# A hybrid decoder layer on one core: stores and side work placed later, groups started one pair of tiles earlier

## The chip, the core and the metric

The kernel runs on one core of a Trainium2 chip. Its engines work at the same time, each through its own instructions in order: TensorE (PE; its weight loads are PEld), VectorE (DVE), ScalarE (ACT), GpSimd (POOL) and SyncE (SP), which here issues the DMA transfers. The metric is device time in microseconds (us); lower is better.

## What is computed

One layer of a decoder over 2048 tokens of width 1024, in float32. After an RMS norm one input projection (1024 to 8320 columns) feeds a recurrent mixer with a matrix state (RWKV-7), a short convolution and a causal pooling over windows of 2, 4, 8 and 16, and three gates for each channel. Each branch is projected, the three are merged by the gates, one output projection follows, then a norm and the residual.

```python
def _rwkv7_step(state, inp):
    r_t, w_t, k_t, v_t, a_t, b_t = inp
    sa = jnp.einsum('bhvk,bhk->bhv', state, a_t)
    state = (state * w_t[:, :, None, :] + sa[..., None] * b_t[:, :, None, :]
             + v_t[..., None] * k_t[:, :, None, :])
    y_t = jnp.einsum('bhvk,bhk->bhv', state, r_t)
    return state, y_t
...
        h = rms_norm(x, pre_norm_w[l])
...
        p = h @ w_cat
        p_rwkv, p_conv, p_pool, p_gate = jnp.split(
            p[..., :N_IN],
            [N_RWKV_IN, N_RWKV_IN + N_CONV_IN, N_RWKV_IN + N_CONV_IN + N_POOL_IN], axis=-1)
        p_rwkv = token_shift(p_rwkv, mu_shift[l])
...
        y_b = short_conv_branch(p_conv, conv_w[l])
        y_c = pool_branch(p_pool, pool_w[l], pool_scale[l])
        ys = jnp.stack([y_a, y_b, y_c], axis=0)
        proj = jnp.einsum('nbsc,ncd->nbsd', ys, w_branch[l])
        gates = jax.nn.sigmoid(p_gate.reshape(bsz, slen, N_BRANCH, D_MODEL))
        merged = jnp.einsum('bsnd,nbsd->bsd', gates, proj)
        out = merged @ w_out[l]
        x = x + rms_norm(out, post_norm_w[l])
```

## The kernel before

Large products are done in float32 accuracy by splitting both operands into a high and a low part, three matmuls for each of four slices, so that one *product* is twelve matmuls of 128x128 by 128x512 (L182 to L184). The weights come as raw pieces by DMA (L149), ScalarE casts the high part (L141), GpSimd subtracts for the low part (L143). The token axis is done in two halves of 1024.

Two tiles of output channels by two blocks of tokens are computed together with seven products in place of eight (the class `Pair`): B11, T1, T2, B21, B22, T3 and T4. T4 is left over to the next pair, where it comes after T1. VectorE evicts with additions at L247 (after B21), L251 (after B22) and L255 (after T3); T4 adds onto the bank that L255 reads, and the next T1 takes the bank that L247 reads. For the sums of weights GpSimd adds (L212).

`execute` runs the program of jobs. A job is a generator that yields after each product; at each yield `supply` prepares coming weights (raw pieces five products ahead, sums three, splits two) and each *side* of the job is advanced by its rate. The jobs: eight pairs and a single tile of projections for the first half (60 products and the low-rank ones, L527 to L529), then for each half eight pairs of the convolution branch (`conv_tile`: a convolution pair, L864 to L869, and a gating pair, L848 and L875), four of pooling (`pool_tile`, additions at L898) and twelve of gates (L950), with the second half's projections after the first half's gates; then eight merge tiles of six products for each half (L981 on VectorE, L985 on GpSimd), and eight pairs of output rows (`out_pair`).

The sides: `rwkv_groups`, eight groups of 128 tokens for each half, each 25 steps long. A group multiplies its chunk matrices (L691, L694, L699), stores a triangle (L704) and loads it by rows (L718), inverts it in 15 pairs of operations (L730, L731) in four batches, one step apart, stores and reloads the result (L738, L740), transposes it (L745, Td), completes the inverse (L753 to L792) and passes the state on (L804 to L833). The following group's head (L561 to L616) and the group before's tail (L624 to L652) run in the same steps. Other sides: `stage_ops` (norm and transposes of the second half's input, L434 to L465), `stage_sums` (L460 to L466), `mix_pooled` (L930 to L943), and the plans that load and split coming operands (L333, L339, L340). `side.finish` runs what is left of a side at once.

PE, DVE, ACT and POOL execute in the order in which the code writes their work; SyncE is not in that list, and its order is the scheduler's:

```python
    with tc.manual_schedule(engines={mybir.EngineType.PE, mybir.EngineType.DVE, mybir.EngineType.Activation,
                                     mybir.EngineType.Pool}):
```

`out_pair` scales a row by its norm and adds the input row (L1023, L1024), for two blocks of 512 columns, once both blocks of the row are there; the norm is three small operations on GpSimd (L470 to L472) after the squares on ScalarE (L1015).

Of the kernel before, what the change touches and what calls it, by code (L numbers as in the profile page):

```python
# [53 lines left out]
def trunk_kernel(ctx, tc, x, pre_norm_w, post_norm_w, w_in, mu_shift, rwkv_w0, rwkv_w_up,  # L54
# [261 lines left out]

    def new_op(o):

        hi = hp_.tile([P, HK, BLK], F32R, tag="hh", name=f"h{o}")
        lo = hp_.tile([P, HK, BLK], F32, tag="hl", name=f"l{o}")  # L320
        return [hi[:, k, :] for k in range(HK)], [lo[:, k, :].bitcast(F32R) for k in range(HK)]
# [104 lines left out]
    def stage_ops(half):  # L426

        for j in range(TH // P):
# [14 lines left out]
            yield  # L443
            for q in range(2):
                t = work("hB")[:, :BLK]
                transposed(xs[q], q, t)
                sp.dma_start(hR[q, b][:, :, c0 * P:(c0 + 1) * P], t.rearrange("p (k t) -> p k t", k=HK))
# [3 lines left out]
    def stage_sums(block, dst):  # L451

        for k in range(2 * HK):
# [7 lines left out]
            yield  # L461
            for o, out_, a, b in (("T1", B[0, 0], B[0, 1], B[0, 0]), ("T3", B[0, 1], B[1, 1], B[0, 1]),
                                  ("T2", B[1, 1], B[1, 1], B[0, 0]), ("T4", B[1, 0], B[1, 0], B[1, 1])):
                dve.tensor_tensor(out_, a, b, ALU.subtract)
                sp.dma_start(dst[o][:, k, cs], out_)  # L465
# [9 lines left out]
    def rwkv_cols(half, c, b, val):  # L475
# [14 lines left out]
        sp.dma_start((rD, kD, vD, zD)[kind][:, i, t0:t0 + BLK], sh)  # L490
# [14 lines left out]
    def rwkv_single(half, h, c):  # L505
# [8 lines left out]
        def sink(b, val):  # L514
# [6 lines left out]
            def products(upw):  # L521
                (uh, ul) = upw
                for n, bias in enumerate((hw0, ha0)):
                    ns = half_of(n)
                    for i in range(NCT):
# [6 lines left out]
                        sp.dma_start(loraD[n][:, i, t0:t0 + BLK], o)  # L532
# [86 lines left out]
    def group_tail(g, by, v):  # L619
# [29 lines left out]
        dve.tensor_tensor(flat(y), flat(y), flat(v), ALU.add)  # L649
        pool.tensor_tensor(flat(y), flat(y), flat(z), ALU.mult)  # L650
        yield
        sp.dma_start(yD[0][:, :, t0:t0 + P], it(y))  # L652
# [10 lines left out]
    def rwkv_group(g, head, before, following):  # L663
# [37 lines left out]

        nd = tc.dram_tile([4, 2 * NCT, 32, 32], F32, name=f"nd{g}")
# [3 lines left out]
        BKs = rp.tile([P, 2, 2 * NCT, 64], F32, tag="BKs", name="BKs")  # L706
        for n in range(2):
            bt = rk_bank()
            quarters(bt, BK[:, n])
            act.copy(BKs[:, n], bt.rearrange("p (a k) -> p a k", k=64))  # L710
            if n:

                ndf = nd.rearrange("q a s t -> (q a) s t")
                NBt = rp.tile([P, 16, 16], F32, tag="BK", name="NB")
                for u in range(2):
                    us = slice(u * 16, u * 16 + 16)
                    for g2 in range(2):
                        sp.dma_start(NBt[(2 * u + g2) * 32:(2 * u + g2) * 32 + 32], ndf[:, us, us])  # L718
                bb = rk_bank()
                for i in range(NCT):  # L720
                    pe.matmul(bb[:, i * P:(i + 1) * P], qones[:, i], it(r)[:, i], start=True, stop=True)
                dve.tensor_tensor(flat(v), bb, flat(v), ALU.mult)
            yield from step()
# [4 lines left out]
        for j in range(15):  # L728
# [122 lines left out]
    def conv_tile(half, h, i):  # L851
# [22 lines left out]
        def gated(e, b, val, _):  # L874
            dve.tensor_tensor(ys[b], ys[b], silu2(val) if e else val, ALU.mult)  # L875
            done.append(b)
            if done.count(b) == 2:
                t0 = half * TH + b * BLK
                sp.dma_start(yD[1][:, i, t0:t0 + BLK], ys[b])
# [3 lines left out]
    def pool_tile(half, h, i):  # L883
        w = WINDOWS[i]

        def sink(e, b, val, u):
            t0 = half * TH + b * BLK
            if e:
                sp.dma_start(yD[2][:, i, t0:t0 + BLK], silu2(val))
# [23 lines left out]
            sp.dma_start(pD[:, i, t0:t0 + BLK], pl[:, :BLK])  # L913
# [3 lines left out]
    def mix_pooled(half):  # L917

        for i in range(NCT):
            pw = work("pw")[:, :P]  # L920
            sp.dma_start(pw, pool_w[i])
            for b in range(NB):
# [20 lines left out]
                sp.dma_start(yD[2][:, i, t0:t0 + BLK], z)  # L943
# [3 lines left out]
    def gate_pair(half, h, n, d):  # L947
        def sink(e, b, val, tile_):
# [3 lines left out]
            sp.dma_start(gD[n][d + e, :, t0:t0 + BLK], t)  # L952
# [10 lines left out]

    def merge_tile(half, ys, d):

        def body():
            acc = [None] * NB
            for n in (1, 2, 0):
                gs = []
                for b in range(NB):  # L970
                    t0 = half * TH + b * BLK
                    gt = work("g")
                    sp.dma_start(gt[:, :BLK], gD[n][d, :, t0:t0 + BLK])
                    gs.append(gt[:, :BLK])
# [11 lines left out]
            for b in range(NB):  # L986
                t0 = half * TH + b * BLK
                sp.dma_start(mD[:, d, t0:t0 + BLK], acc[b])
# [13 lines left out]
    def out_pair(ops, post, j):  # L1002
# [10 lines left out]
        def sink(e, b, val, _):  # L1013
# [5 lines left out]
            for b in range(2):  # L1019
# [216 lines left out]
    def execute(first):  # L1236
        for n, entry in enumerate(program):
# [44 lines left out]
```

## Time and profile before

| | |
|---|---|
| median of three runs | 2371.32 us (2369.45 to 2372.01) |
| the profiled execution | 2369.79 us |
| its span, first to last instruction | 2368.1 us |
| mean granted TensorE clock | 0.952 |
| busy: PE, PEld | 2195.8, 1768.5 us |
| busy: DVE, ACT, POOL | 1403.7, 888.3, 1371.6 us |
| DMA | 313 MB, mean 132 GB/s |

The chip grants TensorE's clock at one of two levels, 2.4 GHz (1.00 in the profile) or 1.2 GHz (0.50); a stretch shows the mean. Busy matmuls are pipelined: at full clock a new one of 512 columns starts every 0.23 us while each is shown with some 0.40 us. A row of a timeline has start, duration, engine, line, operation and tiles; in brackets stands the idle time of that engine before it, and what ended it.

### The profile page before, as it was taken

Reading aid. Unit: us, or ns where it says so; the run is one execution under the profiler, and the core shown is the slowest. Engines: PE = TensorE matmul, PEld = TensorE weight load, DVE = VectorE, ACT = ScalarE, POOL = GpSimd, SP = SyncE. Lnnn points to the kernel's source line nnn. Section 1 sums busy time; section 2 is a strip of 40 time slices with the busy share of each in tenths; the row PEclk is TensorE's granted clock in tenths of the full one; section 3 lists DMA queues with packets and bytes.
Section 4 is the critical chain, followed back from the end, with each engine's and each line's share of the span. In section 5 each row is a group of like instructions: output and inputs, shape, how many; then the busy total and the mean of one; then the engine's idle time right before and its main releaser. Section 6 shows DMA issues by size and latency. Waiting matters only on the chain. (4 is left out here: it accounts for less than half of the span.)

```text
span 2368.1 us, 47007 instructions
## 1 busy us (share of the span) xinstructions
PE 2195.8 (93%) x18514; PEld 1768.5 (75%) x18514; DVE 1403.7 (59%) x2182; ACT 888.3 (38%) x1745; POOL 1371.6 (58%) x1137
## 2 busy tenths in 40 slices
PE   4999989989999998899999998999999898998887
PEld 4788877767787876678877776877777687887775
DVE  7413786777756537554495767766674653527454
ACT  5444432433434345344433333343343311214332
POOL 7567764655646554436775545565574444556774
PEclk7989999999999998889999999999999899999998
DMA  3343322343565336444321323455555746865442
GB/s 101 111 135 119 94 65 74 101 123 101 146 191 158 103 93 203 133 147 140 117 84 54 89 67 99 126 174 148 159 157 177 210 134 176 272 187 183 138 129 71
DMA packets 441207, 313.11 MB, mean 132 GB/s; under 512 B 105557, under 2 KB 362778, under 8 KB 440986
## 3 DMA queue, kind: packets, MB, share of 16 engines
q1 hardware_dynamic: 440986, 310.12, 43.6%
q8 instruction: 145, 2.38, 0.4%
q14 instruction: 76, 0.62, 0.1%
HBM read 206.08 MB, written 103.94 MB: 131 GB/s over the span
## 5 line engine op out<-in xcount | busy, mean ns | idle before, releaser
L143 POOL TENSOR_TENSOR wl<-ws,wh 128x512 fp32r<-128x512 f32 x484 | 680.4, 1409 | 508.5 <-ACT wh L141 489.7
L182 PE MATMUL ch<-hT,wh 128*128 128x512 f32 x864 | 359.3, 416 | 49.9 <-DVE p L255 33.3
L141 ACT CAST wh<-ws 128x512 fp32r<-128x512 f32 x484 | 298.8, 618 | 264.0 <-POOL ws L212 102.8
L183 PE MATMUL ch<-lT,wh 128*128 128x512 f32 x864 | 347.7, 402 | 0.0
L184 PE MATMUL ch<-hT,wl 128*128 128x512 f32 x864 | 347.2, 402 | 0.3 <-POOL wl L143 0.3
L184 PE MATMUL mm<-hB,wl 128*128 128x512 f32 x600 | 238.3, 397 | 8.5 <-POOL wl L143 8.5
L182 PE MATMUL mm<-hB,wh 128*128 128x512 f32 x600 | 244.5, 407 | 1.0 <-ACT p L298 1.0
L182 PEld LDWEIGHTS ch<-hT,wh 128*128 128x128 f32 x864 | 168.8, 195 | 94.6 <-issue 54.6
L183 PE MATMUL mm<-lB,wh 128*128 128x512 f32 x600 | 237.7, 396 | 0.0
L143 POOL TENSOR_TENSOR wl<-s,wh 128x512 fp32r<-128x512 f32 x72 | 97.8, 1358 | 186.5 <-ACT wh L141 175.5
L212 POOL TENSOR_TENSOR ws<-ws,s 128x512 f32<-128x512 f32 x144 | 201.3, 1398 | 0.1
L184 PEld LDWEIGHTS ch<-hT,wl 128*128 128x128 f32 x864 | 168.4, 195 | 38.4 <-POOL wl L143 0.8
L183 PEld LDWEIGHTS ch<-lT,wh 128*128 128x128 f32 x864 | 168.9, 195 | 33.1
L985 POOL TENSOR_TENSOR g<-g 128x512 f32<-128x512 f32 x64 | 87.7, 1374 | 116.0 <-DVE g L981 110.7
L184 PEld LDWEIGHTS mm<-hB,wl 128*128 128x128 f32 x600 | 114.8, 191 | 34.5 <-POOL wl L143 9.4
L182 PEld LDWEIGHTS mm<-hB,wh 128*128 128x128 f32 x600 | 114.8, 191 | 28.1 <-issue 1.5
L182 PE MATMUL mm<-hT,wh 128*128 128x512 f32 x296 | 124.0, 419 | 10.4 <-DVE Ttmp L730 10.4
L183 PEld LDWEIGHTS mm<-lB,wh 128*128 128x128 f32 x600 | 114.8, 191 | 22.6
L184 PE MATMUL ch<-hB,wl 128*128 128x512 f32 x288 | 116.6, 405 | 14.1 <-POOL wl L143 14.1
L182 PE MATMUL ch<-hB,wh 128*128 128x512 f32 x288 | 119.7, 416 | 6.6 <-DVE g L981 4.9
L212 POOL TENSOR_TENSOR ws<-ws 128x512 f32<-128x512 f32 x72 | 104.8, 1456 | 31.3 <-DMA ws<-in_w_in 31.3
L730 DVE TENSOR_TENSOR Ttmp<-NB,Tt 128x120 f32<-128x120 f32 (+14 forms) x240 | 115.4, 481 | 11.0 <-DMA NB<-nd 4.4
(270 smaller groups left out, 4668.1 us busy)
## 6 DMA issues: line engine op xcount, KB each, us to landing
ws<-in_w_in SPq DMA_DIRECT2D x260, 256.0 KB
g<-gD SPq DMA_DIRECT2D x96, 256.0 KB
gD<-p SPq DMA_DIRECT2D x48, 256.0 KB
ws<-in_w_branch SPq DMA_DIRECT2D x48, 256.0 KB
ly<-yD SPq DMA_DIRECT2D x48, 256.0 KB
mD<-g SPq DMA_DIRECT2D x32, 256.0 KB
ws<-mD SPq DMA_DIRECT2D x32, 256.0 KB
xr<-in_x SPq DMA_DIRECT2D x32, 256.0 KB
```

The lines of the kernel that those rows point to most:

```text
L141: act.copy(hi, src)
L143: pool.tensor_tensor(lo, src, hi.bitcast(F32), ALU.subtract)
L182: pe.matmul(bank, hi[:, k, :], th[k], start=start and k == 0, stop=False, skip_group_check=True)
L183: pe.matmul(bank, hi[:, k, :], tl[k], start=False, stop=False, skip_group_check=True)
L184: pe.matmul(bank, lo[:, k, :], th[k], start=False, stop=stop and k == HK - 1, skip_group_check=True)
L212: sums[0].tensor_tensor(w[o], w[a], w[b], op)
L730: dve.tensor_tensor(tmp[:, :, :n], bc(NBt[:, j, j + 1:], 1, 8), bc(Tt[:, :, j], 2, n), ALU.mult)
L985: pool.tensor_tensor(acc[b], acc[b], gs[b], ALU.add)
```

## The change

Stores of computed blocks to DRAM are no longer issued where the data are computed. `store` puts them on a list, and `after_product`, called at every yield, issues the list of the yield before. This goes for the projections, convolution, pooling, gates, merge and output stores and those of the staged operands. `after_product` also runs one piece of work that was put off: in `out_pair` the scaling and addition of a row's block (except for one block whose bank is wanted) is put off, one block at each of the next yields.

In the group the stores of the triangle, its loads, and the stores and loads of the inverse stand in steps of their own. A group keeps 25 steps in the first half and has 24 in the second, where Td comes four steps after the last batch of the inverse in place of five. In the tail the multiplication on GpSimd (L650) moves one step behind VectorE's addition (L649). `stage_ops` has one more step between the scaling (L442) and the transposes, `stage_sums` one between its loads and its subtractions, with rates to match. Four small copies of the inverse (L765, L767) are all on ScalarE.

The groups of the first half start in the last pair of the first projections, those of the second half in the last pair of the second, seven steps earlier each; the pool mixing starts with the third projection job of the second half, at a higher rate. The merge loads its gates one step ahead.

```diff
+    stores, puts = [[], []], []
+    def store(dst, src):
+        stores[1].append((dst, src))
+    def put_off(f):
+        puts.append(f)
+    def after_product():
+        for dst, src in stores.pop(0):
+            sp.dma_start(dst, src)
+        stores.append([])
+        if puts:
+            puts.pop(0)()
...
             for xt in xs:
                 dve.tensor_scalar(xt, xt, ss[:, 3:4], None, ALU.mult)
             yield
+            yield
             for q in range(2):
                 t = work("hB")[:, :BLK]
                 transposed(xs[q], q, t)
-                sp.dma_start(hR[q, b][:, :, c0 * P:(c0 + 1) * P], t.rearrange("p (k t) -> p k t", k=HK))
+                store(hR[q, b][:, :, c0 * P:(c0 + 1) * P], t.rearrange("p (k t) -> p k t", k=HK))
...
         dve.tensor_tensor(flat(y), flat(y), flat(v), ALU.add)
+        yield
         pool.tensor_tensor(flat(y), flat(y), flat(z), ALU.mult)
-        yield
-        sp.dma_start(yD[0][:, :, t0:t0 + P], it(y))
+        store(yD[0][:, :, t0:t0 + P], it(y))
...
+        turned(0)
+        yield from step()
+
         nd = tc.dram_tile([4, 2 * NCT, 32, 32], F32, name=f"nd{g}")
         for q, (qs, bs_) in enumerate(quads):
             sp.dma_start(nd[q].rearrange("a s t -> s a t"), gn[qs, :, bs_])
...
+        turned(1)
+        yield from step()
...
             if j in (3, 7, 11):
                 yield from step()
+        yield from step(1, True)
         tdf = td.rearrange("q a s t -> (q a) s t")
...
+        yield from step()
         for q, (qs, bs_) in enumerate(quads):
             sp.dma_start(TT[qs, :, bs_], td[q].rearrange("a s t -> s a t"))
-        yield from step(5, True)
+        yield from step(3 if g < 8 else 2)
...
-            if q % 2:
-                act.copy(o, i_)
-            else:
-                dve.tensor_copy(o, i_)
+            act.copy(o, i_)
...
+    gate_order = [(half, d, n) for half in range(2) for d in range(KT) for n in (1, 2, 0)]
+    gate_next = []
+    def gates():
+        while gate_order and len(gate_next) < 2:
+            half, d, n = gate_order.pop(0)
+            gs = []
+            for b in range(NB):
+                t0 = half * TH + b * BLK
+                gt = work("g")
+                sp.dma_start(gt[:, :BLK], gD[n][d, :, t0:t0 + BLK])
+                gs.append(gt[:, :BLK])
+            gate_next.append(gs)
+        return gate_next.pop(0)
...
-                dve.scalar_tensor_tensor(o, val, ss[e][:, 3:4], post[0][:, es], ALU.mult, ALU.mult)
-                dve.tensor_tensor(xs[e, b], xs[e, b], o, ALU.add)
-                sp.dma_start(outT[(j + e) * P:(j + e + 1) * P, es], xs[e, b])
+
+                def last(b=b, val=val, o=o, es=es):
+                    dve.scalar_tensor_tensor(o, val, ss[e][:, 3:4], post[0][:, es], ALU.mult, ALU.mult)
+                    dve.tensor_tensor(xs[e, b], xs[e, b], o, ALU.add)
+                    store(outT[(j + e) * P:(j + e + 1) * P, es], xs[e, b])
+
+                if (e, b) == (1, 0):
+                    last()
+                else:
+                    put_off(last)
...
-    mixes = [Side(mix_pooled(0), 24 / 56), Side(mix_pooled(1), 24 / 80)]
-    stages = [Side(stage_ops(1), 64 / 80), Side(stage_sums(wo_block, wD), 16 / 60)]
-    for j in proj(0):
-        job(j)
+    mixes = [Side(mix_pooled(0), 24 / 46), Side(mix_pooled(1), 24 / 80)]
+    stages = [Side(stage_ops(1), 80 / 86), Side(stage_sums(wo_block, wD), 24 / 60)]
+    first = proj(0)
+    for j in first:
+        job(j, *([groups[0]] if j is first[-1] else []))
...
-            for j in proj(1):
-                job(j, side, mixes[0], load)
-            program.append(side.finish)
+            second = proj(1)
+            for n, j in enumerate(second):
+                if n == len(second) - 1:
+                    program.append(side.finish)
+                job(j, side if n < len(second) - 1 else groups[1], *([mixes[0]] if n > 1 else []), load)
             program.append(mixes[0].finish)
...
             for _ in j.run():
                 supply(1)
+                after_product()
                 for side in sides:
                     side.advance()
         if not first:
             for _ in flush():
-                pass
+                after_product()
+            while puts or stores[0] or stores[1]:
+                after_product()
```

## Rows read from the trace of the kernel before

**Rows 1.** Page, part 1: busy us, share of span, instructions.

```profile
PE 2195.8 (93%) x18514; PEld 1768.5 (75%) x18514; DVE 1403.7 (59%) x2182; ACT 888.3 (38%) x1745; POOL 1371.6 (58%) x1137
```

**Rows 2.** Span and mean granted TensorE clock of the core.

```profile
core 0: 2368.1 us, clock 0.952
```

**Rows 3.** Stretches: length, busy PE, PEld, DVE, ACT, POOL; PEclk, DMA.

```profile
405.00:458.00 53.00, 45.63 (x432) 35.89 (x431) 44.44 (x69) 20.91 (x45) 34.20 (x29) 0.90 0.28 79
510.00:560.00 50.00, 37.89 (x362) 30.33 (x361) 39.52 (x74) 16.68 (x37) 25.13 (x30) 0.86 0.31 94
912.00:990.00 78.00, 58.32 (x521) 44.95 (x520) 55.00 (x95) 37.37 (x74) 34.93 (x28) 0.80 0.53 162
1440.00:1482.00 42.00, 32.50 (x329) 25.29 (x328) 32.55 (x55) 14.69 (x31) 23.55 (x18) 0.88 0.28 87
1826.00:1870.00 44.00, 31.13 (x233) 24.38 (x231) 32.84 (x64) 18.79 (x37) 17.16 (x12) 0.81 0.82 251
1998.00:2012.00 14.00, 7.60 (x58) 6.08 (x55) 7.57 (x13) 2.64 (x6) 4.25 (x4) 0.76 0.84 249
2036.00:2044.00 8.00, 6.45 (x30) 5.03 (x29) 8.00 (x11) 0.62 (x1) 3.17 (x3) 1.00 0.97 291
2050.00:2150.00 100.00, 100.00 (x443) 82.81 (x442) 33.30 (x45) 15.99 (x27) 56.48 (x44) 1.00 0.72 206
2186.00:2350.00 164.00, 143.77 (x575) 115.22 (x574) 80.81 (x77) 55.97 (x124) 115.35 (x116) 0.93 0.37 116
```

**Rows 4.** VectorE by line: count | busy us, mean ns | idle before.

```profile
L731 DVE TENSOR_TENSOR Tt<-Tt,Ttmp 128x120 f32<-128x120 f32 (+14 forms) x240 | 117.0, 487 | 8.3
L730 DVE TENSOR_TENSOR Ttmp<-NB,Tt 128x120 f32<-128x120 f32 (+14 forms) x240 | 115.4, 481 | 11.0 <-DMA NB<-nd 4.4
...
L898 DVE TENSOR_TENSOR win<-win 128x525 f32<-128x525 f32 (+2 forms) x24 | 20.8, 867 | 0.8
```

**Rows 5.** Timeline of VectorE, first group: start us, us, line, operation.

```profile
292.63 1.37 DVE L730 TENSOR_TENSOR Ttmp<-NB,Tt 128x120 f32<-128x120 f32 x1
...
314.37 0.68 DVE L247 TENSOR_TENSOR p<-p,mm 128x512 f32<-128x512 f32 x1
```

**Rows 6.** Timeline of PE there.

```profile
315.20 0.64 PE L182 MATMUL mm<-hT,wh 128*128 128x512 f32 x1 [5.19 <-DVE Ttmp L730]
```

**Rows 7.** Timeline of SyncE's queue, merging.

```profile
1996.98 0.50 SPq L1174 DMA_DIRECT2D post<-in_post_norm_w  x1
```

**Rows 8.** Timeline of VectorE, one output pair.

```profile
2237.60 0.74 DVE L1023 SCALAR_TENSOR_TENSOR u<-u,so,post 128x512 f32<-128x512 f32 x1
...
2238.99 0.68 DVE L255 TENSOR_TENSOR p<-p,ch 128x512 f32<-128x512 f32 x1
```

**Rows 9.** Timeline of PE in that pair.

```profile
2239.81 0.47 PE L182 MATMUL ch<-hT,wh 128*128 128x512 f32 x1 [2.79 <-DVE p L255]
```

**Rows 10.** Timeline of PE, end of second half's groups.

```profile
2007.55 0.69 PE L573 MATMUL rk<-ident,d 64*64 64x64 f32 x8 [6.40 <-DVE d L639]
```

**Rows 11.** Waits of POOL: us in total, times, longest us.

```profile
POOL d L650 <- DVE d L649: 62.0, 15, 13.8
...
POOL ws L212 <- DMA ws<-in_w_in: 31.3, 5, 18.8
```

**Rows 12.** Timeline of POOL, second group.

```profile
411.74 1.26 POOL L650 TENSOR_TENSOR d<-d,z 128x512 f32<-128x512 f32 x1 [4.32 <-DVE d L649]
```

**Rows 13.** Timeline of PE, third group.

```profile
524.16 0.45 PE L366 MATMUL rk<-ident,xt 128*128 128x128 f32 x1 [8.93 <-DVE xt L442]
```

**Rows 14.** Timeline of SyncE's queue, seventh group.

```profile
923.11 0.38 SPq L149 DMA_DIRECT2D ws<-in_w_in  x1
934.20 1.80 SPq L738 DMA_DIRECT2D td<-Tt  x4
...
945.33 0.98 SPq L149 DMA_DIRECT2D ws<-in_w_in  x2
```

**Rows 15.** Waits of VectorE: us in total, times, longest us.

```profile
DVE Td L745 <- DMA TT<-td: 19.2, 6, 5.8
```

More of the change, by code (lines that the diff above doesn't have):

```diff
@@ L464, in stage_sums @@
                 dve.tensor_tensor(out_, a, b, ALU.subtract)
-                sp.dma_start(dst[o][:, k, cs], out_)
+                store(dst[o][:, k, cs], out_)
             yield
@@ L489, in rwkv_cols @@
             sh = silu2(sh)
-        sp.dma_start((rD, kD, vD, zD)[kind][:, i, t0:t0 + BLK], sh)
+        store((rD, kD, vD, zD)[kind][:, i, t0:t0 + BLK], sh)
     def rwkv_pair(half, h, c):
@@ L531, in products @@
                         act.activation(o, bank, AF.Tanh, bias=bias[:, i:i + 1], scale=0.5)
-                        sp.dma_start(loraD[n][:, i, t0:t0 + BLK], o)
+                        store(loraD[n][:, i, t0:t0 + BLK], o)
                         if i == 1:
@@ L649, in group_tail @@
         dve.tensor_tensor(flat(y), flat(y), flat(v), ALU.add)
+        yield
         pool.tensor_tensor(flat(y), flat(y), flat(z), ALU.mult)
-        yield
-        sp.dma_start(yD[0][:, :, t0:t0 + P], it(y))
+        store(yD[0][:, :, t0:t0 + P], it(y))
     def rwkv_groups(gs):
@@ L700, in rwkv_group, with turned @@
         quads = [(slice(q * 32, q * 32 + 32), slice(q % 2 * 32, q % 2 * 32 + 32)) for q in range(4)]
+        BKs = rp.tile([P, 2, 2 * NCT, 64], F32, tag="BKs", name="BKs")
+        def turned(n):
+            bt = rk_bank()
+            quarters(bt, BK[:, n])
+            act.copy(BKs[:, n], bt.rearrange("p (a k) -> p a k", k=64))
+        turned(0)
+        yield from step()
         nd = tc.dram_tile([4, 2 * NCT, 32, 32], F32, name=f"nd{g}")
@@ L704, in rwkv_group @@
             sp.dma_start(nd[q].rearrange("a s t -> s a t"), gn[qs, :, bs_])
[L706 to L723, printed above, removed]
+        turned(1)
+        yield from step()
+        ndf = nd.rearrange("q a s t -> (q a) s t")
+        NBt = rp.tile([P, 16, 16], F32, tag="BK", name="NB")
+        for u in range(2):
+            us = slice(u * 16, u * 16 + 16)
+            for g2 in range(2):
+                sp.dma_start(NBt[(2 * u + g2) * 32:(2 * u + g2) * 32 + 32], ndf[:, us, us])
+        bb = rk_bank()
+        for i in range(NCT):
+            pe.matmul(bb[:, i * P:(i + 1) * P], qones[:, i], it(r)[:, i], start=True, stop=True)
+        dve.tensor_tensor(flat(v), bb, flat(v), ALU.mult)
         Tt = rp.tile([P, 8, 16], F32, tag="sa", name="Tt")
@@ L878, in gated @@
                 t0 = half * TH + b * BLK
-                sp.dma_start(yD[1][:, i, t0:t0 + BLK], ys[b])
+                store(yD[1][:, i, t0:t0 + BLK], ys[b])
         return [in_pair(h, col(1), col(2), conv), in_pair(h, col(0), col(3), gated)]
@@ L888, in sink @@
             if e:
-                sp.dma_start(yD[2][:, i, t0:t0 + BLK], silu2(val))
+                store(yD[2][:, i, t0:t0 + BLK], silu2(val))
                 return
@@ L912, in sink @@
             dve.scalar_tensor_tensor(pl[:, o:BLK], cur[:, 16 + o:], 1.0 / w, u[:, 16 + o:], ALU.mult, ALU.subtract)
-            sp.dma_start(pD[:, i, t0:t0 + BLK], pl[:, :BLK])
+            store(pD[:, i, t0:t0 + BLK], pl[:, :BLK])
         return in_pair(h, OFF_POOL + i * P, OFF_POOL + 512 + i * P, sink)
@@ L942, in mix_pooled @@
                 dve.scalar_tensor_tensor(z, bk, qps[:, i:i + 1], z, ALU.mult, ALU.mult)
-                sp.dma_start(yD[2][:, i, t0:t0 + BLK], z)
+                store(yD[2][:, i, t0:t0 + BLK], z)
                 yield
@@ L951, in sink @@
             t0 = half * TH + b * BLK
-            sp.dma_start(gD[n][d + e, :, t0:t0 + BLK], t)
+            store(gD[n][d + e, :, t0:t0 + BLK], t)
         return in_pair(h, OFF_GATE + n * D + d * P, OFF_GATE + n * D + (d + 1) * P, sink)
@@ L968, in body @@
             for n in (1, 2, 0):
[L969 to L974, printed above, removed]
+                gs = gates()
                 w = take()
@@ L987, in body @@
                 t0 = half * TH + b * BLK
-                sp.dma_start(mD[:, d, t0:t0 + BLK], acc[b])
+                store(mD[:, d, t0:t0 + BLK], acc[b])
         return Other([w_block(w_branch[n], 0, d * P) for n in (1, 2, 0)], body)
```

## The prediction

> **What bounds the kernel now.** I read the page's busy line first: TensorE is busy for 2195.8 us [rows 1] of a span of 2368.1 [rows 2], so it is the bound, and what can be won is its idle time (172.3 us) and the time in which its clock was granted at half (1.2 instead of 2.4 GHz). The table of stretches gives both: I call *loss* of a stretch its length minus PE busy, plus (1 - granted clock) x length. Undisturbed, the loss is nil: 100 us of merging with PE busy throughout at clock 1.00, 443 matmuls, so a product of twelve takes 2.71 us [rows 3]. With the mean clock of 0.952 [rows 2] the whole span loses 172.3 + 114 = 286 us. Part of it lies in the start, the low-rank products and the end, which the change hardly touches; of the rest most sits in a few places of [rows 3]: 405 to 458 loses 7.4 + 5.3 = 12.7, 510 to 560 12.1 + 7.0 = 19.1, 912 to 990 19.7 + 15.6 = 35.3, 1440 to 1482 9.5 + 5.0 = 14.5, 1826 to 1870 12.9 + 8.4 = 21.3, 1998 to 2012 6.4 + 3.4 = 9.8, and the output stage, 2186 to 2350, 20.2 + 11.5 = 31.7. An idle time of 1.55 us left the clock at 1.00 (2036 to 2044); the output stage's, 2.8 each, came with 0.93 [rows 3].
>
> Why TensorE waits is read from the timelines. VectorE is only 59% busy, but in bursts: one inverse is 30 small operations, 240 + 240 recorded ones taking 117.0 + 115.4 us, 14.5 us for each of sixteen groups [rows 4]. They stand in VectorE's order before the evictions L247, L251 and L255, whose banks TensorE needs two to three products later. First group: the burst starts at 292.63, L247 runs at 314.37 [rows 5], and TensorE, idle for 5.19 us, starts at 315.20 [rows 6].
>
> **The change part by part.**
>
> *Stores.* They are written one to two products later, but SyncE is not among the engines whose order is kept as written. The load of the post-norm weights is written at the first step of the last two merge tiles, 19 products (52 us) before the stretch from 2186 on, so near 2134; SyncE issued it at 1996.98 [rows 7]. So a transfer goes when its inputs are ready in the scheduler's plan, and a store written later falls behind only what is ready at the same moment. I cost the stores, the gate loads one step ahead, and the transfers of the inverse in their own steps at nil; ends -12 us (rival 2) and +12 (a buffer held one product of 2.71 longer than its next user can wait, at some four places). Who waits in SyncE's order meanwhile: weight loads.
>
> *Output rows.* In each pair VectorE scales and adds two halves of a row (L1023, L1024, twice) before L255; TensorE's T4 product waits for L255. The second half begins at 2237.60 and L255 at 2238.99 [rows 8]; T4 starts at 2239.81 after 2.79 us idle [rows 9]. With the second half behind L255, L255 comes 1.39 us earlier, idle time falls to 1.4. If the clock then holds, as it did after 1.55, the half-clock share goes too: 31.7 / 7 pairs = 4.5 us each become 1.6 (1.4 and a chain that catches up 0.2); if not, 3.1. I take 2.2: 7 x -2.3 = -16 (-10 to -22). The moved half is done 1.4 us after L255, and the next row starts over 8 us later, so it hides. The last T4 gains -1.4.
>
> *End of the second half's groups.* Before, they get 168 + 42 steps and need 11 + 8 x 25 + 9 = 220; the rest is run at once at 1998 to 2012, where TensorE waits 6.40 for the last normalisation [rows 10]. After, they start seven steps earlier and need 11 + 8 x 24 + 9 = 212 of 217: the whole 9.8 goes (if steps slip, half of it: ends -9.8 and -5).
>
> *L650 one step later.* GpSimd waits 62.0 us for L649 in all [rows 11], once 4.32 [rows 12], with the weights' low part L143 queued behind it, for which TensorE waits in turn. One product (2.7) later most of the wait is gone. What is late next is the burst itself. 405 to 458: 12.7 to 10, -3 (-8 to +3).
>
> *Transposes one step later.* At 515 TensorE waits 8.93 us for L442 behind the burst [rows 13]. One product later it waits less, but L255 ran right after L442, so T4 is late next. The burst also moves from pooling tile 1 to tile 0, with one window addition (0.87 us [rows 4]) less per block. 19.1 to 11: -8 (-15 to -3). The mirror in the second half, 14.5 to 9: -5.5 (-10 to +3).
>
> *Starting one pair earlier* moves all bursts by seven products, in the second half by one more per group. (a) 912 to 990: SyncE stood from 923.11 to 934.20 behind the store of a late inverse; the next weight load went out at 945.33 [rows 14] and GpSimd waited 18.8 us for weights [rows 11]. There the burst met the splitting of the next half's operands and the pool mixing; both now come after it. But the splitting still falls on the group's next steps: 35.3 to 18, -17 (-27 to -5). (b) 1826 to 1870, the same meeting with the first merge tile: 21.3 to 8, -13 (-20 to -3). (c) First group of both halves: in the middle of the burst now come two convolutions of four operations instead of one gating of two; at 0.87 each [rows 4] 7.0 us instead of 1.7, less some 2 us since the burst can start sooner: +3 each, +6 (0 to +16). (d) Fourth group of the second half: now at pooling tile 3 (four additions per block). From the burst to L255: 24 operations x 0.48 + 8 additions x 0.87 + six others at 0.87 = 23.7; TensorE has five products, 13.6, and VectorE some 2 us of lead: 8 us idle and, as beside the first group's 5.19, some 3 for the clock: +11. Nil is the lower end, 1.37 us for each operation as at 292.63 [rows 5] the upper: 24 x 0.89 = 21 more, +32.
>
> The Trainium skill, "SBUF — State Buffer", section "SBUF: two separate sides", says that VectorE with two SBUF inputs and GpSimd take a shared port in turn, the loser blocked for the whole instruction. By it the upper end of (d) would be the rule wherever GpSimd is kept busy, and rival 3 the forecast. The mean of 0.48 beside the single 1.37 shows that here it holds for some operations only.
>
> *One step less before Td in the second half.* Td (L745) waited 19.2 us for its transfer, in six waits [rows 15]; the step taken away is 2.7 us in eight groups, of which I let a quarter reach TensorE: +5 (0 to +12).
>
> *Mixing moved to the low-rank tile*, beside the eighth inverse: +4 (-3 to +10). *Four copies from VectorE to ScalarE*: nil, 0.3 us each behind 14.5 us bursts.
>
> **Sum** on the profiled execution (2368.1 span, 2369.8 us): -16 - 1.4 - 9.8 - 3 - 8 - 5.5 - 17 - 13 + 6 + 11 + 5 + 4 = -47.7, so 2322; the median of the runs stands 1.5 above the profiled one: **2323.6 us**.
>
> **The rivals.**
> 1. *Bursts only move*: what is won at 912 and 1826 is lost elsewhere. Then output, end of groups and the last T4 alone remain: -27, 2344. For it: (c) and (d). Against: 912 and 1826 were meetings of three kinds of work.
> 2. *Stores do leave SyncE's way*: the scheduler puts them behind the weight loads, and the rest of GpSimd's 31.3 us of waits for weights [rows 11] vanishes too: 31.3 - 18.8 = 12 more, 2311. Against: [rows 7].
> 3. *Slower: the bursts at convolution and pooling tiles run at the dear price.* Seven inverses meet such tiles (first three groups of the first half, first four of the second). Before, the first group's 24 took 21.7 us from 292.63 to 314.37 with 4 us of other work in between, 0.75 each, for 5.19 idle. At 1.37 they take 15 more; half of it stays, as an idle TensorE soon leaves GpSimd without work: 7.5 each, 52 in all: 2376. It decides from 47 / 7 = 6.7 us each. For it: [rows 5]; against: the mean in [rows 4], which holds both prices.
> 4. *It doesn't do what it says* for the stores is my forecast.
>
> **How the numbers follow.** Forecast 0.62 (2295 to 2345 by itself), rival 1 0.17, rival 2 0.10, rival 3 0.08, others 0.03. The range 2288 to 2360 leaves out rival 3 and the far ends. About 0.2% (4.7 us) is what a measurement can tell: faster 0.88, same 0.04, slower 0.08.
>
> **What would show it.** Right: idle before T4 in the output stage near 1.4 at clock about 1.00; no stretch like 1998 to 2012; GpSimd's wait for L649 far below 62 us in all; no 18 us wait for weights; SyncE's waits on stores much as before. Wrong: a new idle time above 15 us beside pooling tile 3 of the second half, first groups above 10 us each, or TensorE waiting for Td in most groups of the second half.

## The result, and the profile after

The changed kernel takes 2333.9 us (median; 2332.7 to 2334.0), the kernel before 2371.0 beside it: a ratio of 0.984, 95% interval 0.983 to 0.986. That is 37 us won; 47.7 were forecast (2323.6), and the time lies in the range. The sum was nearly right, but the experiments show that its terms were not: one part that I costed at nothing wins, by itself, as much as the whole change.

The page of the changed kernel, busy times, and its span and clock:

```profile
PE 2188.3 (94%) x18514; PEld 1763.1 (76%) x18514; DVE 1371.5 (59%) x2150; ACT 893.7 (38%) x1777; POOL 1364.3 (58%) x1137
```

```profile
core 0: 2332.2 us, clock 0.960
```

TensorE's idle time fell from 172.3 to 143.9 us, the half-clock share from 114 to 93 [rows 1, 2]. The stretches that answer to [rows 3] (length; busy PE, PEld, DVE, ACT, POOL; granted clock; DMA; loss is length minus PE busy, plus one minus clock, times length):

```profile
395.00:415.00 20.00, 17.62 (x187) 13.23 (x188) 17.43 (x20) 10.93 (x22) 16.29 (x11) 0.91 0.38 103
485.00:532.00 47.00, 38.88 (x364) 30.82 (x363) 40.29 (x70) 17.79 (x40) 27.91 (x27) 0.89 0.34 101
900.00:950.00 50.00, 40.64 (x517) 31.69 (x516) 40.16 (x53) 30.70 (x64) 27.78 (x21) 0.93 0.57 183
970.00:1030.00 60.00, 51.59 (x392) 37.23 (x392) 24.79 (x63) 27.26 (x52) 17.48 (x15) 0.77 0.49 151
1488.00:1525.00 37.00, 27.27 (x243) 21.75 (x242) 27.04 (x50) 11.98 (x25) 15.61 (x14) 0.77 0.47 141
1826.00:1870.00 44.00, 43.81 (x511) 35.48 (x510) 30.33 (x48) 18.45 (x36) 15.45 (x12) 1.00 0.78 245
2162.00:2316.00 154.00, 137.18 (x570) 109.12 (x568) 80.37 (x77) 55.17 (x124) 114.94 (x116) 0.97 0.39 123
```

The meeting at the end of the first half's gates now loses 12.9 us (35.3 before), the one with the first merge tile 0.2 (21.3), the transposes 13.3 (19.1), the second group, at 395, 4.2 (12.7), the seven output pairs 21.4 (31.7). New are 18.2 us at pooling tile 3 of the second half, and the low-rank tiles lose 22.2 in place of some 10. In TensorE's timeline the last pair of the second projections begins 17.9 us earlier than before, the second merge tile of the second half 24.3, the end 35.9. By stages that is -17.9, -6.4 and -11.6, where the forecast's terms add up to -21, -9.3 and -17.4. So far it looks like a forecast with every term a little too large. It wasn't.

Two more views of the changed kernel. GpSimd's waits (us in total, times, longest), and three idle times of TensorE (in brackets, with what ended them):

```profile
POOL d L671 <- DVE d L669: 26.1, 9, 5.7
...
POOL ws L212 <- DMA ws<-in_w_in: 4.1, 2, 2.8
```

```profile
1499.63 0.76 PE L182 MATMUL ch<-hT,wh 128*128 128x512 f32 x1 [7.01 <-DVE p L255]
1516.36 0.86 PE L779 MATMUL rk<-Td,G 16*32 16x32 f32 x49 [2.73 <-DVE Td L771]
1900.40 0.74 PE L779 MATMUL rk<-Td,G 16*32 16x32 f32 x64 [2.20 <-DVE Td L771]
```

The first is the burst of the fourth group at pooling tile 3, the others are two of the second half's waits for Td, which has one step less there: TensorE waits for it in six of the eight groups, 0.7 to 4.0 us each. Before, it waited for Td three times in all, 5.0 us together.

### The profile page after: what moved, and what is told of

It is laid out like the page before. It is cut to its first block, busy times and chain, and to the rows that moved or that the text cites. A ratio compares the mean times of both kernels' runs of the same rounds, so it can differ in the third digit from the quotient of the medians.

```text
span 2332.2 us, 46983 instructions
## 1 busy us (share of the span) xinstructions
PE 2188.3 (94%) x18514; PEld 1763.1 (76%) x18514; DVE 1371.5 (59%) x2150; ACT 893.7 (38%) x1777; POOL 1364.3 (58%) x1137
## 4 chain that ended last, share of the span: by engine, by line
PE 61%; DVE 15%; issue 6%; POOL 6%; ACT 3%; DMA 3%; SPq 2%; POOLq 0%; DVEq 0%; ACTq 0%
PE ch L182 9%; PE ch L183 8%; PE ch L184 8%; PE mm L182 7%; PE mm L183 7%; PE mm L184 7%; DVE Tt L755 3%; DVE Ttmp L754 3%; POOL wl L143 3%; PE rk L711 2%; PE rk L593 2%; POOL ws L212 1%; PE rk L835 1%; PE rk L827 1%; PE rk L843 1%
## 5 line engine op out<-in xcount | busy, mean ns | idle before, releaser
L143 POOL TENSOR_TENSOR wl<-ws,wh 128x512 fp32r<-128x512 f32 x484 | 672.5, 1392 | 555.0 <-ACT wh L141 516.0
L212 POOL TENSOR_TENSOR ws<-ws,s 128x512 f32<-128x512 f32 x144 | 201.7, 1400 | 0.0
L184 PEld LDWEIGHTS mm<-hB,wl 128*128 128x128 f32 x600 | 112.7, 188 | 24.3
L184 PE MATMUL mm<-hT,wl 128*128 128x512 f32 x296 | 120.5, 407 | 1.1 <-POOL wl L143 0.8
L755 DVE TENSOR_TENSOR Tt<-Tt,Ttmp 128x120 f32<-128x120 f32 (+14 forms) x240 | 115.3, 480 | 8.3
```

Source lines behind the costliest of these rows:

```text
L143: pool.tensor_tensor(lo, src, hi.bitcast(F32), ALU.subtract)
L184: pe.matmul(bank, lo[:, k, :], th[k], start=False, stop=stop and k == HK - 1, skip_group_check=True)
L212: sums[0].tensor_tensor(w[o], w[a], w[b], op)
L755: dve.tensor_tensor(Tt[:, :, j + 1:], Tt[:, :, j + 1:], tmp[:, :, :n], ALU.add)
```

## Experiments

Times are medians, ratios are to the kernel before, run beside each; the changed kernel stands at 0.984 (0.983 to 0.986).

**One part alone, on the kernel before**

*The output rows.*

```diff
-                dve.scalar_tensor_tensor(o, val, ss[e][:, 3:4], post[0][:, es], ALU.mult, ALU.mult)
...
+                if (e, b) == (1, 0):
+                    last()
+                else:
+                    puts.append(last)
```

> The kernel before with one part of the change alone: in the output pairs the scaling and addition of a row's block are put off, one block at each of the next products; stores stay immediate. Theory A (each idle time is paid with the half clock that follows it, as forecast): -16 -1.4 = -17, so 2354 us. Theory B (an output pair is a loop L255 -> T4 -> norm on GpSimd -> L1023 -> L247 -> L255, whose length alone sets the pace, whatever the clock does): the loop loses the 1.39 us of one block, eight times, so -11 and 2360 us, with T4 of successive pairs 22.4 us apart instead of 23.8.

2358.3 us, 0.995 (0.993 to 0.996): -11.8, as the loop says. The T4 products of two successive pairs, in that run:

```profile
2236.99 0.47 PE L182 MATMUL ch<-hT,wh 128*128 128x512 f32 x1 [1.38 <-DVE p L255]
...
2259.36 0.77 PE L182 MATMUL ch<-hT,wh 128*128 128x512 f32 x1 [2.63 <-DVE p L255]
```

They are 22.4 us apart, whether TensorE idled 1.38 or 2.63 us; before it was 23.8. The changed kernel shows why the forecast's accounting fails here. Four successive output pairs of it, from T4 to T4:

```profile
2188.32:2210.74 22.42, 20.97 (x85) 16.86 (x85) 11.68 (x12) 8.13 (x19) 16.97 (x17) 0.92 0.46 141
2210.74:2233.13 22.39, 19.65 (x84) 15.61 (x85) 11.65 (x12) 7.92 (x19) 16.95 (x17) 0.99 0.46 141
2233.13:2255.57 22.44, 20.82 (x85) 16.76 (x85) 11.69 (x12) 8.13 (x19) 17.00 (x17) 0.93 0.47 141
2255.57:2277.98 22.41, 19.66 (x85) 15.62 (x85) 11.64 (x12) 7.92 (x19) 16.96 (x17) 1.00 0.45 141
```

A pair with the clock at 0.92 is as long as one at 1.00: where TensorE is slower it only waits less for the same VectorE instruction. Idle time and half clock can't be added up where another engine sets the pace.

*L650 one step later.*

```diff
-        pool.tensor_tensor(flat(y), flat(y), flat(z), ALU.mult)
         yield
+        pool.tensor_tensor(flat(y), flat(y), flat(z), ALU.mult)
```

> The kernel before with one part alone: in a group's tail the multiplication L650 on GpSimd stands one step behind VectorE's addition L649; the number of steps stays. Forecast: GpSimd's 62 us of waiting for L649 go for the most part, and TensorE gains 3 us at 405 to 458 and as much at the like place of the second half, 2364 to 2368. If the wait of GpSimd is what TensorE pays there: 7.7 and 6.0 us at the two places, 2357. If it only moves: 2371 within 2.

2368.9 us, 1.000 (0.999 to 1.001): nothing. The stretch at 405 loses 2.7 us less, the one at 510 1.7 more, and GpSimd still waits 54.3 us for L649.

*The group's own steps.*

```diff
+        turned(0)
+        yield from step()
+
         nd = tc.dram_tile([4, 2 * NCT, 32, 32], F32, name=f"nd{g}")
...
+        yield from step(1, True)
         tdf = td.rearrange("q a s t -> (q a) s t")
...
+        yield from step()
         for q, (qs, bs_) in enumerate(quads):
             sp.dma_start(TT[qs, :, bs_], td[q].rearrange("a s t -> s a t"))
-        yield from step(5, True)
+        yield from step(3)
...
+            act.copy(o, i_)
```

> The kernel before with one part alone: in each group the store and load of the triangle and of the inverse stand in steps of their own, the sums behind the load (the multiplication of v on VectorE too) come one step later, and the four small copies go to ScalarE; 25 steps as before. Forecast: nil, 2369 within 4. If this part is what made the first half shorter (the run with the groups started as before still lost 4 us less at the first group and 5 less at 725): -5 to -12, 2357 to 2364.

2332.0 us, 0.984 (0.982 to 0.985): -38, as much as the whole change. At the end of the first half's gates SyncE's queue reads, in this run:

```profile
923.02 0.98 SPq L149 DMA_DIRECT2D ws<-in_w_in  x2
925.38 0.89 SPq L743 DMA_DIRECT2D td<-Tt  x2
```

Before, the store of the inverse stood ahead of these two weight loads [rows 14]: SyncE waited 10.6 us for the late inverse and sent them at 945.33. Now they go first, 2.4 us before its first part. The stretch, and the first group's place in TensorE's timeline:

```profile
900.00:960.00 60.00, 49.86 (x451) 38.62 (x450) 53.73 (x90) 35.95 (x74) 32.81 (x24) 0.89 0.66 201
```

```profile
312.07 0.47 PE L182 MATMUL mm<-hT,wh 128*128 128x512 f32 x1 [1.19 <-ACT wh L141]
...
316.44 0.47 PE L182 MATMUL ch<-hT,wh 128*128 128x512 f32 x1 [1.39 <-DVE p L255]
```

The stretch loses 16.7 us in place of 35.3. At the first group TensorE idles 1.19 + 1.39 in place of 5.19 [rows 6] and the clock stays up; before, it read:

```profile
308.00:320.00 12.00, 6.81 (x23) 5.17 (x22) 9.59 (x21) 2.54 (x5) 4.88 (x4) 0.86 0.10 17
```

So 2.6 us are lost instead of 6.9, and 2.6 instead of 8.6 at its like in the second half. Of the 37 us by which TensorE's timeline runs ahead before the output stage, 14 come up at the end of the gates, 9 at the two first groups, the rest in pieces of up to 4 us at other groups.

At the first group of all, neither the inverse's store nor the copies can be the cause: TensorE gains its 4 us there before that group's inverse is stored, and no group ran before it. VectorE's order is what differs. Before:

```profile
288.26 0.69 DVE L722 TENSOR_TENSOR v<-rk,v 128x512 f32<-128x512 f32 x1 [2.08 <-PE rk L721]
288.87 0.68 DVE L255 TENSOR_TENSOR p<-p,ch 128x512 f32<-128x512 f32 x1
```

and in this run, whose TensorE is 0.9 us later there:

```profile
286.94 0.68 DVE L255 TENSOR_TENSOR p<-p,ch 128x512 f32<-128x512 f32 x1
...
291.86 0.69 DVE L727 TENSOR_TENSOR v<-rk,v 128x512 f32<-128x512 f32 x1 [0.29 <-PE rk L726]
```

L255 no longer stands behind the multiplication of v and its wait. The 24 operations of the burst before L247 then take 18.4 us in place of 21.7: 10 of them last over 0.9 us, 13 before. How the rest divides over the three edits, the later multiplication of v, the later transfers and the copies, was not taken apart; nor does SyncE's wait at the inverse's store measure the gain: it falls from 76.5 us to 53.0 here, but is 76.5 again in the run with the groups started as before (below), which is as fast.

*Staging and mixing.*

```diff
                 dve.tensor_scalar(xt, xt, ss[:, 3:4], None, ALU.mult)
             yield
+            yield
...
-    mixes = [Side(mix_pooled(0), 24 / 56), Side(mix_pooled(1), 24 / 80)]
-    stages = [Side(stage_ops(1), 64 / 80), Side(stage_sums(wo_block, wD), 16 / 60)]
+    mixes = [Side(mix_pooled(0), 24 / 46), Side(mix_pooled(1), 24 / 80)]
+    stages = [Side(stage_ops(1), 80 / 86), Side(stage_sums(wo_block, wD), 24 / 60)]
```

> The kernel before with two parts that act at different places: the staging of the second half's operands with one more step before its transposes and its subtractions (440 to 840 and 900 to 930), and the pool mixing two pairs later at the higher rate (912 to 1060). Forecast: -8 at 510 to 560, +4 for the mixing at the low-rank tile, the meeting at 912 to 990 (35 us lost) left for the most part: 2365. If later mixing and staging mend the meeting, as the run with the groups started as before suggests (22 lost there): -8 -13 +4 = -17, 2352.

2380.4 us, 1.004 (1.003 to 1.006): slower by 10. The transposes do gain (510 to 560 loses 14.2 in place of 19.1), but two rows of TensorE's timeline show what takes it back and what stays:

```profile
750.60 0.64 PE L755 MATMUL rk<-Td,G 16*32 16x32 f32 x30 [6.66 <-DVE Td L747]
```

```profile
958.68 0.79 PE L184 MATMUL ch<-hB,wl 128*128 128x512 f32 x1 [10.60 <-POOL wl L143]
```

In the first VectorE stood 8.7 us at the staging's subtractions, which waited for their load, with L247 and Td behind them; with its half clock it costs 10 us, and the place lost 1 before. The second is the meeting of 912 to 990: still there (33 us lost), so the later mixing doesn't mend it. The low-rank tiles lose 5 us more.

*Stores one product later.*

```diff
-                sp.dma_start(mD[:, d, t0:t0 + BLK], acc[b])
+                store(mD[:, d, t0:t0 + BLK], acc[b])
```

> The kernel before with one part alone: the stores of computed blocks one product behind their data (gate loads, groups and rows as before). If they win by letting the inverse's transfers and the weight loads pass, as the run with immediate stores showed for the changed kernel (9 us): -4 to -10, 2359 to 2365, seen at 912 to 990, where a store of the late inverse stood ahead of weight loads, or in VectorE's waits for Td. If they matter only where Td has one step less: 2369 within 3.

2370.0 us, 1.000 (0.999 to 1.001): nothing, as forecast.

**One part taken out of the changed kernel**

*Stores at once.*

```diff
-        stores[1].append((dst, src))
+        sp.dma_start(dst, src)
```

> The kernel after, with every store issued where its data are computed instead of one product later; all else, the order on the other four engines too, is as in after. If the putting off of stores does nothing (forecast): 2334 us within 3. If it takes stores out of the way of the weight loads (rival 2): some 12 us come back, 2346 us, and GpSimd's waits for weights at L212 rise from 4 us towards the 31 of before.

2342.8 us, 0.989 (0.987 to 0.990): 9 to 10 us slower. So the stores do bring something here, though alone they don't. SyncE's queue around the last inverse, with stores at once (there the stores' line is L321, here L329):

```profile
1896.92 0.56 SPq L321 DMA_DIRECT2D yD<-d  x1
1897.58 0.58 SPq L763 DMA_DIRECT2D td<-Tt  x1
1899.43 0.32 SPq L321 DMA_DIRECT2D mD<-g  x1
1899.80 1.45 SPq L763 DMA_DIRECT2D td<-Tt  x3
1901.30 1.41 SPq L998 DMA_DIRECT2D g<-gD  x3
1902.87 1.80 SPq L766 DMA_DIRECT2D TT<-td  x4
```

and in the changed kernel:

```profile
1890.76 1.80 SPq L763 DMA_DIRECT2D td<-Tt  x4
...
1894.55 2.00 SPq L766 DMA_DIRECT2D TT<-td  x4
```

With stores at once a merge store slips between the four parts of the inverse's store, and SyncE waits for its data; the reload goes 5.3 us after the first store instead of 3.8. TensorE then waits 4.78 us for Td in place of 2.20, in all 22.3 in place of 15.0. GpSimd's waits for weights at L212 rise too, from 4.1 to 11.0 us. Of the 9.9 us that the profiled spans differ by, 1.5 have come up by the last pair of the second projections, the rest in the second half's groups, much of it at Td.

*The step before Td given back* to five groups of the second half.

```diff
-        yield from step(3 if g < 8 else 2)
+        yield from step(3 if g < 13 else 2)
```

> The kernel after, with five of the eight groups of the second half (the first five) given back the step before Td; all 217 steps are then used. If the missing step is what TensorE pays at Td (the idle times before L779 and the half clock behind them, 15 us in these five groups), and the fourth group's burst, three products later, leaves the last pooling tile (12 us, a half of it): -15 to -21, so 2313 to 2319 us. If bursts only move: 2330 to 2338. Forecast's own price of the step (+5 for all eight): -3, 2331.

2326.2 us, 0.981 (0.980 to 0.983): -8, between the forecast's price (-3) and the -15 that the idle times at Td with their half clock seemed to be worth. TensorE's waits for Td fall from 15.0 to 5.7 us; but the burst of the fourth group, three products later, still costs 9.4 (12.1 before its Td in the changed kernel):

```profile
1512.74 0.79 PE L182 MATMUL ch<-hT,wh 128*128 128x512 f32 x1 [6.03 <-ACT u L243]
```

*Groups started as before.*

```diff
-        job(j, *([groups[0]] if j is first[-1] else []))
+        job(j)
```

(and the second half's groups with its first convolution pair)

> The kernel after, with the groups of both halves started where the kernel before starts them (seven products later, and 210 steps for the 212 of the second half). By the forecast's terms the earlier start was worth -17 -13 at the two meetings and -9.8 at the end of the groups, and cost +6 +11 and part of 5 at other places: without it 20 to 30 us come back, 2354 to 2364. If bursts only move (rival 1): 2334 within 6. If the meetings were mended by the stores instead: 2340 or less.

2330.0 us, 0.983 (0.982 to 0.985): the same as with the earlier start, or 2 to 4 us less. Rival 1 holds for this part: bursts only move. The two meetings, in this run:

```profile
895.00:945.00 50.00, 36.68 (x306) 27.73 (x305) 42.37 (x67) 28.60 (x59) 27.33 (x20) 0.83 0.55 168
...
1805.00:1825.00 20.00, 6.32 (x55) 4.31 (x57) 6.41 (x10) 4.45 (x8) 3.82 (x3) 0.66 0.97 289
```

They lose 21.8 and 20.5 us; with the earlier start 12.9 and 0.2. That gain of 29 is more than given back: 15 at the two first groups (11.5 + 11.8 us in place of 3.6 + 4.3), 12 at pooling tile 3 and the wait for Td behind it (18.3 in place of 6.5), 8 at the low-rank tiles (22 in place of 14), 7 at the wait for Td of the seventh group, whose inverse met the merge tile before, less some 8 in smaller gains of other groups. The finish of 9.8 at the end of the groups is gone in this run too (from 1955 to 1990 TensorE loses nothing): the 24 steps do that, not the start.

*Mixing as before.*

```diff
-    mixes = [Side(mix_pooled(0), 24 / 46), Side(mix_pooled(1), 24 / 80)]
+    mixes = [Side(mix_pooled(0), 24 / 56), Side(mix_pooled(1), 24 / 80)]
...
-                job(j, side if n < len(second) - 1 else groups[1], *([mixes[0]] if n > 1 else []), load)
+                job(j, side if n < len(second) - 1 else groups[1], mixes[0], load)
```

> The kernel after, with the pool mixing of the first half started with the second half's first projection pair and at the old rate, as in the kernel before. If it is the mixing that made the low-rank stretch dearer (21 us lost there after, 10 before): -5 to -11, 2323 to 2329 us, unless it is lost again beside the splitting of operands, where before lost 35. If the eighth group's inverse, now there seven products earlier, is the cause: 2334 within 3. Forecast's price of the mixing at this place: +4, so 2330.

2333.7 us, 0.985 (0.984 to 0.987): nothing, and the low-rank tiles lose 22 us (970 to 1030) as with the later mixing. 8 us of that are the earlier start's, as seen above: the eighth group's inverse now falls on them.

**The output stage taken further**

*The first row's blocks behind L255* as well (one empty entry ahead of them).

```diff
+                    if (e, b) == (0, 0):
+                        put_off(lambda: None)
                     put_off(last)
```

> The kernel after, with both blocks of a pair's first row behind L255 (one product later than the change puts them). Theory B: another 1.77 + 1.67 = 3.4 us leave the loop, which falls from 22.4 to 19.0 us, just the seven products of 2.72 us each: 7 x -3.4 = -24, so about 2310 us, no idle time before T4 and no half clock in the output stage. Theory A: the gaps left in the output stage with their half clock, 22 us, go too: 2312. Rival: GpSimd, busy for 16 us of each pair, becomes the bound with its alternation with ScalarE: at least half of the gain stays away, 2322 or more.

2318.8 us, 0.978 (0.976 to 0.980): -15, not -24. A pair takes 21.2 us. Three engines hand on the delay, GpSimd first, then VectorE and ScalarE, then GpSimd again:

```profile
2216.27 0.55 POOL L492 TENSOR_TENSOR so<-so,mhalf 128x1 f32<-128x1 f32 x1
```

```profile
2216.86 0.75 DVE L1059 SCALAR_TENSOR_TENSOR o<-ch,so,post 128x512 f32<-128x512 f32 x1 [4.75 <-POOL so L492]
...
2221.96 0.68 DVE L247 TENSOR_TENSOR p<-p,mm 128x512 f32<-128x512 f32 x1
```

```profile
2222.73 0.63 ACT L1049 ACTIVATE junk<-p 128x512 bf16<-128x512 f32 x1 [6.57 <-DVE p L247]
```

```profile
2224.04 1.29 POOL L143 TENSOR_TENSOR wl<-ws,wh 128x512 fp32r<-128x512 f32 x1 [2.55 <-ACT wh L141]
```

VectorE does the second row's two blocks (5.1 us) before L247; ScalarE's square waits for L247 with the weight cast behind it; GpSimd waits for the cast, and its next norm comes late.

*All blocks behind the evictions.*

```diff
                 if (e, b) == (1, 0):
-                    last()
-                else:
-                    put_off(last)
+                    put_off(lambda: None)
+                    put_off(lambda: None)
+                put_off(last)
```

> The kernel after, with the blocks of a pair's second row behind L247 and L251 of the next pair, so that no eviction of VectorE stands behind a block any more (the first row's blocks then follow L255). In the run with the first row's blocks behind L255 a pair still took 21.2 us: GpSimd finished the second row's norm (L492) late, VectorE did that row's blocks before L247, ScalarE's casts stood behind the squares of L247's block, and GpSimd waited for the casts. If that loop is the bound: it is cut here, and a pair takes its products' time, 19.0 to 19.6 us, 7 x -2.8 to -3.4 against after, so 2310 to 2314 us. If GpSimd's own work sets the pace (16.4 us of operations for each pair, 1.3 to 1.7 us each): no better than 21.2, 2319 us or more.

2308.7 us, 0.974 (0.973 to 0.976): -25. L247 now waits for its product alone, and a pair takes the 19.1 us of its seven products, GpSimd being busy for 18.8 of them:

```profile
2211.80 0.69 DVE L247 TENSOR_TENSOR p<-p,mm 128x512 f32<-128x512 f32 x1 [4.78 <-PE mm L184]
```

```profile
2203.35:2222.49 19.14, 19.14 (x85) 15.77 (x84) 13.82 (x12) 8.37 (x18) 18.80 (x18) 1.00 0.50 165
```

*The best of these together:* the rows as above, the step before Td for five groups, and the first half's groups started as before.

```diff
-        yield from step(3 if g < 8 else 2)
+        yield from step(3 if g < 13 else 2)
...
+                    put_off(lambda: None)
+                    put_off(lambda: None)
+                put_off(last)
...
-        job(j, *([groups[0]] if j is first[-1] else []))
+        job(j)
```

> The kernel after with three edits: all blocks of the output rows behind the evictions (-25 us by itself), the step before Td given back to five groups of the second half (-8 by itself), and the groups of the first half started where the kernel before starts them (that run stood 4 us lower than after at the end of the first half). If the three add, as they act at different places: 2333.9 - 25 - 8 - 4 = 2297 us; if the first half's start only moves: 2301.

2294.2 us, 0.968 (0.966 to 0.969): the three add, and 40 us are won on the changed kernel. The group's steps and the output rows alone, without the other parts of the change, were not run together.

## Why the prediction was right, and where it was not

**The sum.** The single parts measured on the kernel before (rows -11.8, L650 -0.4, group steps -37.7, staging and mixing +10.7, stores +0.3) add up to -39; the whole change gives -37. What is left, the earlier start, the 24 steps and the gate loads, comes to about nothing as far as parts add. In TensorE's timeline the same shows at the second merge tile of the second half: the run with the group's steps alone stands 36.9 us ahead of the kernel before, the changed kernel 24.3. Up to there the rest of the change costs 12.6 us, and the output rows win about as much behind it.

**Stores, gate loads and the inverse's transfers at nil: the step that failed.** I put three things into one term. The stores alone are nil, as said; the gate loads were not tried alone. The group's own steps are -38. The argument was that SyncE's order is the scheduler's, so that a step later in the text changes nothing. But [rows 14] showed a store of a late inverse ahead of weight loads, and with the group's steps they pass it, which is worth some 14 us there. I read that row for the earlier start, and didn't ask what the step at the store itself would do to it. And the sums behind the triangle's load had no term at all, though the multiplication of v moves in VectorE's order, where the forecast looked for its waits. "SyncE's waits on stores much as before" was to show the forecast right; at the inverse's store they fall from 76.5 us to 50.3. Of the other 23 us, 9 come up at the two first groups, where VectorE's order differs; where the rest comes from stays open.

**(a) and (b), -17 and -13, and (c) and (d), +6 and +11.** The sizes came out near (-22 and -21; +6 and +12), the reason didn't. At (a) the group's steps alone bring the loss from 35.3 to 16.7, so most of it isn't the earlier start's. (b) is: 17 us are lost there with the group's steps alone, 20 in the changed kernel with the old start, but 7 of them come back at the same group's wait for Td. (c) was sized on the first groups of before, which with their waits for Td lose 17.5 us together; with the group's steps and the old start they lose 8, so that the earlier start costs 15 there, not 6. (d) is the forecast's mechanism and size: 12.1 us, 7.01 idle and the half clock beside it. Together the earlier start is worth nothing.

**End of the groups, -9.8:** it came (from 1984 to 2001 the changed kernel loses nothing), by the 24 steps. **Td's step, +5,** is their price: five of eight groups give 8 us when they get it back, so it is dearer than the forecast. **Mixing, +4:** nil in the changed kernel; of the loss at the low-rank tiles (+12) 8 came with the earlier start, which the forecast had not costed there.

**Transposes, -8 and -5.5:** the first stretch gains 5 to 6, its mirror in the second half 8 in the changed kernel (6.2 in place of 14.5), but on the kernel before the staging with its new rates, tried together with the mixing, costs 10. The new rates were not costed: VectorE then waits at a subtraction for its load, with evictions queued behind it.

**L650, -3:** nil. GpSimd's wait fell from 62.0 [rows 11] to 54.3 with that edit alone, and to 26.1 in the whole change; TensorE didn't pay for it.

**Output rows, -16 and -1.4:** -11.8. The mechanism was right, one block of 1.39 us leaves the way of L255 in each of eight pairs: 11.1. The step that failed is "if the clock then holds, the half-clock share goes too". The pair is a loop through four engines and its length doesn't depend on the clock; and idle time didn't fall to 1.4 but to 1.4 and 2.6 by turns.

**The rivals.** Rival 1 is what the earlier start did, though not the time it gave (2344), because the gain came from elsewhere. Rival 2 fails as stated, since stores alone give nothing; its 12 us are near the 9 to 10 that they give once the inverse's transfers have little slack, but GpSimd's waits for weights, which were to make them up, account for 7 us at most. Rival 3 did not come about: the seven groups at such tiles lose 70 us together, 73 before, where it asked for 52 more.

**The signs.** No stretch like 1998 to 2012 and no long wait for weights is left, and GpSimd waits 26.1 us for L649, as the forecast wanted. The idle time before T4 and SyncE's waits are not as it wanted. Of its signs of being wrong, TensorE's waits for Td in most groups of the second half did come; the first groups lose over 10 us each, 6.0 and 6.7 of it idle; pooling tile 3 stays below 15 us idle (9.7). So that the sum came near is in part luck: the gain of the group's steps, costed at nil, stands where the earlier start was to win and wins nothing in sum.

## What to carry to other kernels

A term costed at nil needs the same question as the large ones: which row shows this instruction waiting, and who is queued behind it there; here a group's steps, costed at nil, were worth as much as the whole change. Where successive rounds take the same time at different clocks, look for the loop through the other engines and count only what leaves it. Moving a burst by a few tiles mends the meeting that one sees and makes others that one doesn't: sum both before believing either.

## What the runs showed of the hardware

VectorE's small operations have two prices, and GpSimd decides which. In the kernel before, of the 480 of the inverse 119 take over 0.9 us (148.7 us together) and 361 take 0.23 us on average. The long ones lie beside a GpSimd operation for 97% of their time, the short ones for 10%. The first group of before, GpSimd and then VectorE:

```profile
303.68 1.74 POOL L212 TENSOR_TENSOR s<-ws 128x512 f32<-128x512 f32 x1
305.38 1.30 POOL L143 TENSOR_TENSOR wl<-ws,wh 128x512 fp32r<-128x512 f32 x1
307.88 1.29 POOL L143 TENSOR_TENSOR wl<-s,wh 128x512 fp32r<-128x512 f32 x1 [1.20 <-ACT wh L141]
```

```profile
305.57 1.22 DVE L731 TENSOR_TENSOR Tt<-Tt,Ttmp 128x88 f32<-128x88 f32 x1
306.82 0.24 DVE L730 TENSOR_TENSOR Ttmp<-NB,Tt 128x80 f32<-128x80 f32 x1
307.10 0.24 DVE L731 TENSOR_TENSOR Tt<-Tt,Ttmp 128x80 f32<-128x80 f32 x1
...
307.92 1.33 DVE L730 TENSOR_TENSOR Ttmp<-NB,Tt 128x64 f32<-128x64 f32 x1
```

While GpSimd works, each of these small operations of VectorE takes as long as one of GpSimd's; in its pause from 306.68 to 307.88 they take 0.24. GpSimd pays too: 1.74 in place of 1.29. So the mean of 0.48 that the forecast used is a mean of two prices, and the 1.37 of rival 3 is the ordinary price beside a busy GpSimd. This agrees with the Trainium skill, "SBUF — State Buffer", section "SBUF: two separate sides", which tells of a lock on a shared port, held for a whole instruction.
